# Low-rank products of an RWKV-7 layer in fp32 on two row tiles, two PSUM copies moved to ScalarE, and a new order of the whole layer

## The chip, the core and the metric

The kernel runs on one NeuronCore of a Trainium2 chip. The metric is the device time of one execution in microseconds. The kernel before took 1311.3 us as the median of 3 runs (1308.73 to 1313.69).

## What is computed

Two decoder layers run on one prompt of 512 tokens and on eight samples of 4 tokens, all in fp32, with weights shared by both. Layer 0, the one that the change touches, is RWKV-7 time mixing. Cut to what matters:

```python
proj = h @ w_in                                  # 1024 -> 8320 columns: r, k, v, wd, ad, z
xm = sh + (prev - sh) * mu                       # token shift
wf = w0 + jnp.tanh(wd) @ w2                      # low-rank product, 64 -> 2048
a = jax.nn.sigmoid(a0 + ad @ a2)                 # low-rank product, 64 -> 2048
decay = jnp.exp(-jnp.exp(-jax.nn.softplus(-wf) - 0.5))
# per head (32 heads of 64), token after token:
#   S = S*decay + (S @ -kk) (kk*a)^T + v k^T ;  y = S r
o = (groupnorm(y) + bonus) * jax.nn.silu(z)
out = o @ w_out
```

Layer 1 is a gated MLP (projections, a causal 128 by 128 mixing, an output projection); the change leaves it alone.

## The kernel before, in words

**Layout.** Features lie on partitions and tokens on columns. The 544 tokens are two halves of 272 columns (256 of the prompt and 16 of the samples, `HT`). Most fp32 products are made as three products of rounded halves (`mm3`, lines 249 to 252: high by high, high by low, low by high), each one TensorE instruction of 272 columns.

**Steps.** The 2048 mixer features are 16 tiles of 128 (two heads each). Step `p` of the loop projects k, r, v, z of tile `p`: four projections of 16 units, a unit being one `mm3`, so 64 units of three products a step (`units`, L375). Between the units stand the small products of the recurrence, taken from three tiles at once: low-rank products and Gram matrices of tile `p` or `p+1`, the chunk algebra of `p-1` (`lanes`, `merge`, `chain`, `sample`), the group norm of `p-2` (`tail`).

**The order is written out.** Each generator (`lora`, `kpost`, `chain`, ...) yields after each piece. The table `AT` (L1066) gives every piece a place `u`, counted in units from the start of its step; `agenda` sorts all pieces of all steps by `64 * p + u`, and inside the manual schedule every engine and the DMA queue of SP issue their instructions in exactly that order. A place of 115.1 thus means: in the step after, behind unit 51. `BANKS` says in which PSUM bank a product lands: `wa` is two banks used in turn, `sm`, `g`, `s`, `y` are one each; the projections have two of their own (`pp`), and a half of a projection can start only when the half before the last one has been read by ScalarE (`shift`, pieces 1 and 2, L392 and L393).

**What the change and the prediction touch.**

- `lora_in` (L413) rounds tanh(wd) and ad to high and low halves and stacks them on 128 partitions (`lw`, `la`). `lora(p)` (L432) loads the two 64 by 128 weights twice each, one copy below the other, rounds them (L442 on ScalarE), makes the low halves (L446, twice on VectorE), and then runs, for each half of the tokens and each of w and a, two products of 128 rows and 272 columns (L453, L454) with a tanh out of PSUM behind each pair (L457, L458). Pieces 11 to 14 are the `l1` copy, the VectorE scan L473, and the exponentials Ep and Em.
- `merge(p)` copies the product `pak` into ZR by VectorE (L752). `chain(p)` copies `pz` into XA in four pieces, two by VectorE (L843) and two by ScalarE (L841).
- `chain` then makes `pa` (L858) and `pn` (L864), adds the identity (L876), forms ND (L879) and RT (L885), and runs a serial loop of seven products `sb` (L889), each followed by one VectorE update of the state (L891) that the next one needs.
- `sample` has the products `psm` (L939 to L944), `pit` (L969), `psy` (L975) and `pst`/`psu` (L987): the last are two fp32 products of 64 rows and 256 columns on partitions 0 to 63 and 64 to 127. `gram` (L580) likewise pairs fp32 products of 64 rows and 128 columns.
- `flip` (L795) turns a block of the input for the residual; for its ninth call (k = 8) the sample rows are loaded.

Of the kernel before, what the change touches and what calls it, by code (L numbers as in the profile page):

```python
# [29 lines left out]
BANKS = {'plw0': 'wa', 'plw1': 'wa', 'pla0': 'sm', 'pla1': 'sm', 'pss': 'wa', 'pge0': 'y', 'pge1': 's', 'pgo0': 'wa', 'pgo1': 'wa', 'pbo0': 'sm', 'pbo1': 's', 'pbk0': 'wa', 'pbk1': 'wa', 'pv': 'wa', 'pat': 'sm', 'pak': 'y', 'pxt': 'wa', 'psu': 'wa', 'pm1': 'g', 'pm2': 's', 'pm3': 'wa', 'pm4': 'sm', 'ps0': 'wa', 'pit': 'wa', 'psy': 's', 'pst': 'sm', 'pso': 's', 'psm': 'wa'}  # L30
# [36 lines left out]
def build(tc, A, O, off):  # L67
# [5 lines left out]
    with ctx:  # L73
# [335 lines left out]
        lw = lH.tile([128, 2, HT], F32R, name="lw")  # L409
        la = lH.tile([128, 2, HT], F32R, name="la")  # L410
        xl = hd("xl", "h1")

        def lora_in():  # L413
            xlc, ll = (hd(n, t)[:, cl].rearrange("p (h j) -> p h j", h=2) for n, t in (("xlc", "h3"), ("ll", "h7")))
            parts = [(slice(0, 256), xl[:, 0:512].rearrange("p (h j) -> p h j", h=2)), (slice(256, 272), xl[:, 512:544].rearrange("p (h j) -> p h j", h=2))]
            for js, src in parts:
# [1123 lines left out]
```

## Time and profile before

| what | value |
|---|---|
| median of 3 runs | 1311.3 us (1308.73 to 1313.69) |
| the profiled execution, its own time | 1309.46 us |
| its span, first to last instruction | 1307.7 us |
| mean granted TensorE clock | 0.993 |
| TensorE matmul busy | 1266.9 us (97%) |
| VectorE busy | 991.5 us (76%) |
| ScalarE busy | 678.4 us (52%) |
| GpSimd busy | 158.4 us (12%) |
| DMA moved | 124.31 MB, mean 95 GB/s |

Busy shares are means over stages. The stage of the 16 steps fills the time from about 30 to 740 us; the output projection and layer 1 follow. Busy TensorE time counts the whole length of pipelined products, which overlap; the distance from one start to the next tells what a product costs in the stream. A row of the timeline ends, where the engine had been idle, with that idle time and what ended it, in brackets. TensorE's granted clock is 1.00 (2.4 GHz) except in a few short stretches at 0.50 (1.2 GHz).

### The profile page before, as it was taken

How to read it: one execution, taken by the hardware profiler on the slowest of the kernel's cores; microseconds unless marked ns; L12 is line 12 of the kernel's file. 1: busy time of each engine (PE TensorE's matmuls, PEld its weight loads, DVE VectorE, ACT ScalarE, POOL GpSimd, SP SyncE). 2: the span in 40 equal slices, each digit the busy share in tenths (PEclk: the TensorE clock that was granted, in tenths of full speed). 3: DMA queues.
4: the chain of work that ended last, by engine and by line, in shares of the span. 5: the costliest groups of instructions: out<-in, count | busy, mean ns of one | idle time of the engine just before them, and what ended most of it. 6: DMA issues, size and time to landing. Idle time of an engine off the chain costs nothing.

```text
span 1307.7 us, 35973 instructions
## 1 busy us (share of the span) xinstructions
PE 1266.9 (97%) x14860; PEld 1207.7 (92%) x14860; DVE 991.5 (76%) x2314; ACT 678.4 (52%) x1583; POOL 158.4 (12%) x350
## 2 busy tenths in 40 slices
PE   6989999999999999999999889999999999999997
PEld 5989999999999998999989779999999999999997
DVE  5779999999999998999989877374448656556466
ACT  5666576656766765666666453253333323233333
POOL 1112121121212111221212100000000000000000
PEclk9989999999999999999999999999999999999999
DMA  4424243434434342433323464433222232231511
GB/s 155 120 59 102 68 110 97 101 89 107 102 77 112 86 108 78 109 81 91 83 69 97 115 177 115 118 98 88 81 81 83 64 106 76 61 115 53 161 36 70
DMA packets 279785, 124.31 MB, mean 95 GB/s; under 512 B 114643, under 2 KB 272485, under 8 KB 279621
## 3 DMA queue, kind: packets, MB, share of 16 engines
q1 hardware_dynamic: 259972, 106.93, 30.5%
q10 hardware_dynamic: 19648, 15.08, 3.9%
q8 instruction: 117, 1.92, 0.6%
q14 instruction: 48, 0.39, 0.1%
HBM read 102.02 MB, written 19.95 MB: 93 GB/s over the span
## 4 chain that ended last, share of the span: by engine, by line
PE 71%; DVE 16%; ACT 6%; issue 3%; DMA 2%; POOL 2%; DVEq 0%; SPq 0%; POOLq 0%; ACTq 0%
PE r_p L250 3%; PE gz_p L250 3%; PE r_p L251 3%; PE r_p L252 3%; PE gz_p L252 2%; PE gu_p L250 2%; PE gz_p L251 2%; PE gu_p L252 2%; PE gu_p L251 2%; PE gv_p L251 2%; PE gv_p L252 2%; PE gv_p L250 2%; PE pgo L580 2%; PE po L250 2%; PE po L252 2%
## 5 line engine op out<-in xcount | busy, mean ns | idle before, releaser
L250 PE MATMUL r_p<-hh,r_h 128*128 128x272 f32 x256 | 79.4, 310 | 8.8 <-ACT raw L393 8.8
L395 POOL COPY shl<-raw 128x9 f32<-128x9 f32 x49 | 27.0, 552 | 497.8 <-ACT raw L393 487.8
L250 PE MATMUL z_p<-hh,z_h 128*128 128x272 f32 x256 | 80.3, 314 | 0.0
L250 PE MATMUL v_p<-hh,v_h 128*128 128x272 f32 x256 | 79.9, 312 | 0.0
L250 PE MATMUL k_p<-hh,k_h 128*128 128x272 f32 x256 | 77.6, 303 | 0.0
L250 PE MATMUL gv_p<-hh,gv_h 128*128 128x272 f32 x256 | 75.6, 295 | 0.0
L250 PE MATMUL gz_p<-hh,gz_h 128*128 128x272 f32 x256 | 75.5, 295 | 0.0
L251 PE MATMUL r_p<-hl,r_h 128*128 128x272 f32 x256 | 74.8, 292 | 0.0
L252 PE MATMUL r_p<-hh,r_l 128*128 128x272 f32 x256 | 74.7, 292 | 0.0
L252 PE MATMUL v_p<-hh,v_l 128*128 128x272 f32 x256 | 74.4, 291 | 0.0
L251 PE MATMUL v_p<-hl,v_h 128*128 128x272 f32 x256 | 74.3, 290 | 0.0
L250 PE MATMUL gu_p<-hh,gu_h 128*128 128x272 f32 x256 | 74.2, 290 | 0.0
L251 PE MATMUL gv_p<-hl,gv_h 128*128 128x272 f32 x256 | 74.2, 290 | 0.0
L252 PE MATMUL gv_p<-hh,gv_l 128*128 128x272 f32 x256 | 74.1, 289 | 0.0
L252 PE MATMUL k_p<-hh,k_l 128*128 128x272 f32 x256 | 74.0, 289 | 0.0
L251 PE MATMUL gu_p<-hl,gu_h 128*128 128x272 f32 x256 | 73.9, 289 | 0.0
L252 PE MATMUL gu_p<-hh,gu_l 128*128 128x272 f32 x256 | 73.9, 289 | 0.0
L252 PE MATMUL gz_p<-hh,gz_l 128*128 128x272 f32 x256 | 73.9, 289 | 0.0
L252 PE MATMUL z_p<-hh,z_l 128*128 128x272 f32 x256 | 73.8, 288 | 0.0
L251 PE MATMUL gz_p<-hl,gz_h 128*128 128x272 f32 x256 | 73.7, 288 | 0.0
L251 PE MATMUL k_p<-hl,k_h 128*128 128x272 f32 x256 | 73.7, 288 | 0.0
L251 PE MATMUL z_p<-hl,z_h 128*128 128x272 f32 x256 | 73.6, 288 | 0.0
(441 smaller groups left out, 4729.4 us busy)
## 6 DMA issues: line engine op xcount, KB each, us to landing
k_r<-rw_in SPq DMA_DIRECT2D x16, 512.0 KB
r_r<-rw_in SPq DMA_DIRECT2D x16, 512.0 KB
v_r<-rw_in SPq DMA_DIRECT2D x16, 512.0 KB
z_r<-rw_in SPq DMA_DIRECT2D x16, 512.0 KB
gv_r<-gm_in SPq DMA_DIRECT2D x16, 512.0 KB
gu_r<-gm_in SPq DMA_DIRECT2D x16, 512.0 KB
gz_r<-gm_in SPq DMA_DIRECT2D x16, 512.0 KB
go_r<-gm_out SPq DMA_DIRECT2D x24, 256.0 KB
```

The source lines that it names most:

```text
L250: T.matmul(ps, whi, ahi, start=first, stop=False)
L251: T.matmul(ps, whi, alo, start=False, stop=False)
L252: T.matmul(ps, wlo, ahi, start=False, stop=last)
L395: G.tensor_copy(shl[:, :, f], raw[:, 512:553:5])
L580: T.matmul(pg[h][:, 128 * j : 128 * j + 128], BK[rs, c].rearrange("p a b -> p (a b)"), AR[rs, :, c, :], start=True, stop=True)
```

## The change

The low-rank products become plain fp32: the weights are loaded once each, w2 on partitions 0 to 63 and a2 on 64 to 127, without rounding; for each half of the tokens one product of 64 rows and 272 columns is made for w and one for a, from the two row halves of TensorE into two banks. XA leaves PSUM by ScalarE alone, ZR too. All places and all banks of small products are new; the projections and everything after the steps stay as they were. The core of the diff (of the places, the lines that the prediction speaks of):

```diff
-BANKS = {'plw0': 'wa', 'plw1': 'wa', 'pla0': 'sm', 'pla1': 'sm', 'pss': 'wa', 'pge0': 'y', 'pge1': 's', 'pgo0': 'wa', 'pgo1': 'wa', 'pbo0': 'sm', 'pbo1': 's', 'pbk0': 'wa', 'pbk1': 'wa', 'pv': 'wa', 'pat': 'sm', 'pak': 'y', 'pxt': 'wa', 'psu': 'wa', 'pm1': 'g', 'pm2': 's', 'pm3': 'wa', 'pm4': 'sm', 'ps0': 'wa', 'pit': 'wa', 'psy': 's', 'pst': 'sm', 'pso': 's', 'psm': 'wa'}
+BANKS = {'plw0': 'wa', 'plw1': 'g', 'pla0': 'sm', 'pla1': 's', 'pss': 'g', 'pge0': 'g', 'pge1': 'wa', 'pgo0': 's', 'pgo1': 'wa', 'pbo0': 's', 'pbo1': 'g', 'pbk0': 'g', 'pbk1': 's', 'pv': 'y', 'pat': 'wa', 'pak': 'sm', 'pxt': 'sm', 'psu': 'wa', 'pm1': 'y', 'pm2': 'wa', 'pm3': 'sm', 'pm4': 'sm', 'ps0': 'wa', 'pit': 'wa', 'psy': 'sm', 'pst': 's', 'pso': 'wa', 'psm': 'y'}
...
-        lw = lH.tile([128, 2, HT], F32R, name="lw")
-        la = lH.tile([128, 2, HT], F32R, name="la")
+        lx = lH.tile([128, 2, HT], F32, name="lx")
         xl = hd("xl", "h1")
         def lora_in():
-            xlc, ll = (hd(n, t)[:, cl].rearrange("p (h j) -> p h j", h=2) for n, t in (("xlc", "h3"), ("ll", "h7")))
-            parts = [(slice(0, 256), xl[:, 0:512].rearrange("p (h j) -> p h j", h=2)), (slice(256, 272), xl[:, 512:544].rearrange("p (h j) -> p h j", h=2))]
-            for js, src in parts:
-                S.activation(xlc[e_, :, js], src[e_], AF.Tanh)
-            S.activation(lw[e_], xlc[e_], AF.Copy)
-            V.tensor_tensor(out=ll[e_], in0=xlc[e_], in1=lw[e_], op=ALU.subtract)
-            for js, src in parts:
-                S.activation(la[o_, :, js], src[o_], AF.Copy)
-                V.tensor_tensor(out=ll[o_, :, js], in0=src[o_], in1=la[o_, :, js], op=ALU.subtract)
-            for rs, os, x in ((e_, o_, lw), (o_, e_, la)):
-                S.activation(x[os], ll[rs], AF.Copy)
-            yield
-
-        lrls = [lH.tile([128, 2, 128], F32R, name=f"lrl{i}") for i in range(2)]
-        for x in lrls:
-            G.memset(x[o_, 0, :].bitcast(F32), 0.0)
-            G.memset(x[e_, 1, :].bitcast(F32), 0.0)
+            for js, src in ((slice(0, 256), xl[:, 0:512].rearrange("p (h j) -> p h j", h=2)), (slice(256, 272), xl[:, 512:544].rearrange("p (h j) -> p h j", h=2))):
+                S.activation(lx[e_, :, js], src[e_], AF.Tanh)
+                S.activation(lx[o_, :, js], src[o_], AF.Copy)
+            yield
         def lora(p):
             z = Z[p]
-            pb = slice(128 * p, 128 * p + 128)
-            lr = lH.tile([128, 2, 128], F32, name=f"lr{p}", tag="lr", bufs=1)
-            for i, n in enumerate(("rw_w2", "rw_a2")):
-                w = A[n][0, :, pb]
-                Q.dma_start(lr[:, i, :], bass.AP(w.tensor, w.offset, [[0, 2]] + [list(x) for x in w.ap]))
-            yield
-            lrh = lH.tile([128, 2, 128], F32R, name=f"lrh{p}", tag="lrh", bufs=2)
-            S.activation(lrh, lr, AF.Copy)
-            yield
-            lrl = lrls[p % 2]
-            for i, rs in enumerate((e_, o_)):
-                V.tensor_tensor(out=lrl[rs, i, :], in0=lr[rs, i, :], in1=lrh[rs, i, :], op=ALU.subtract)
-            yield
-            xa = z["xa"] = hd(f"xa{p}", "h1")
-            pw, pa = [None] * 2, [None] * 2
-
-            def down(h, i, x, ps):
-                ps[h] = bk(f"pl{'wa'[i]}{h}", p)[:, 0:HT]
-                T.matmul(ps[h], lrh[:, i, :], x[:, h, :], start=True, stop=False)
-                T.matmul(ps[h], lrl[:, i, :], x[:, h, :], start=False, stop=True)
-
-            def tanh(h, ps, dp_, ds_, bcol):
-                S.activation(dp_[:, 4 * h : 4 * h + 4, :], ps[h][:, 0:256].rearrange("p (c j) -> p c j", j=64), AF.Tanh, bias=bcol, scale=0.5)
-                S.activation(ds_[:, 4 * h : 4 * h + 4, :], ps[h][:, 256:272].rearrange("p (c j) -> p c j", j=4), AF.Tanh, bias=bcol, scale=0.5)
-
+            lr = lH.tile([128, 128], F32, name=f"lr{p}", tag="lr", bufs=2)
+            for n, rs in (("rw_w2", e_), ("rw_a2", o_)):
+                Q.dma_start(lr[rs], A[n][0, :, 128 * p : 128 * p + 128])
+            yield
             for h in range(2):
-                down(h, 0, lw, pw)
-                yield
-                tanh(h, pw, pv(xw), sv(xw), pcol(w0h, p))
-                yield
-                down(h, 1, la, pa)
-                yield
-                tanh(h, pa, cpv(xa), csv(xa), pcol(w0h, 16 + p))
-                yield
+                ps = [bk(f"pl{n}{h}", p)[:, 0:HT] for n in "wa"]
+                for x, rs in zip(ps, rw_):
+                    T.matmul(x, lr[rs], lx[rs, h, :], start=True, stop=True)
+                yield
+                if h == 0:
+                    xa = z["xa"] = hd(f"xa{p}", "h1")
+                for x, dp_, ds_, bcol in ((ps[0], pv(xw), sv(xw), pcol(w0h, p)), (ps[1], cpv(xa), csv(xa), pcol(w0h, 16 + p))):
+                    S.activation(dp_[:, 4 * h : 4 * h + 4, :], x[:, 0:256].rearrange("p (c j) -> p c j", j=64), AF.Tanh, bias=bcol, scale=0.5)
+                    S.activation(ds_[:, 4 * h : 4 * h + 4, :], x[:, 256:272].rearrange("p (c j) -> p c j", j=4), AF.Tanh, bias=bcol, scale=0.5)
+                    yield
...
-            V.tensor_copy(right(p)[:, :, 64:128], pk.rearrange("p (j k) -> p j k", k=64))
+            S.activation(right(p)[:, :, 64:128], pk.rearrange("p (j k) -> p j k", k=64), AF.Copy)
...
-                    if h:
-                        S.activation(XA[rs, h::2, :], c128(pz[a])[hs, :, 0:64], AF.Copy)
-                    else:
-                        V.tensor_copy(XA[rs, h::2, :], c128(pz[a])[hs, :, 0:64])
+                    S.activation(XA[rs, h::2, :], c128(pz[a])[hs, :, 0:64], AF.Copy)
...
-            sk=(14.7847, 15.8601, 16.324, 16.6354, 16.6354, 16.6354, 16.6354),
+            sk=(0.789221, 8.8031, 15.711, 15.8424, 17.6719, 17.7726, 18.4403),
-            bonus=(55.0395, 55.0395, 79.713, 79.713, 79.713, 79.713),
+            bonus=(47.1621, 50.0087, 67.1245, 68.9711, 69.0871, 71.7472),
-            sides=(73.8815, 76.9425, 82.4769, 90.6529, 90.874),
+            sides=(71.9966, 73.0768, 73.0768, 79.7128, 89.332),
-            lora=(-53.3437, -35.604, -22.0198, -6.51455, -6.51455, -5.67349, 1.68797, 1.68797, 5.54808, 5.54808, 6.00962, 7.83685, 9.52597, 14.6652, 14.6652, 18.0281),
+            lora=(-37.6497, -16.243, -12.6778, -6.32377, -6.32377, -5.15096, 0.12609, 0.958916, 8.84795, 19.5291, 19.5291, 39.8259),
-            merge=(80.6858, 90.1492, 90.1492, 91.3358, 93.8559, 94.4782, 95.4232, 98.4293, 102.797, 103.005, 103.005),
+            merge=(89.9516, 90.29, 91.6755, 91.6755, 93.2448, 94.0464, 94.0464, 99.0064, 99.0064, 102.136, 102.373),
-            smp=(12.838, 64.6761, 72.7011, 73.1509, 74.2051, 74.2051, 74.2051, 74.713, 75.2658, 76.703, 76.8464, 76.8464, 78.0988, 90.3058, 91.8793, 93.8484, 93.9934, 93.9934, 95.368, 98.3682, 100.668, 102.567, 110.18, 111.216, 111.216, 126.326, 133.839, 137.039, 155.339),
+            smp=(4.36649, 64.2531, 73.5271, 79.3115, 79.3115, 82.6169, 82.6169, 82.6169, 84.1463, 84.509, 88.3156, 89.5629, 89.5629, 90.1406, 90.873, 93.3779, 94.0364, 99.466, 102.52, 102.958, 103.396, 105.645, 115.209, 116.915, 116.947, 124.943, 129.788, 136.306, 191.625),
-            chain=(103.35, 103.492, 104.192, 104.192, 104.45, 104.45, 104.45, 106.129, 107.734, 110.12, 110.344, 110.344, 110.344, 110.344, 110.983, 110.983, 111.461, 111.99, 111.99, 116.223, 116.571, 118.245, 119.291, 120.662, 122.737, 122.737, 123.448, 124.261, 126.451, 128.474, 134.567, 137.125, 137.125, 137.16, 138.698, 138.698, 151.352, 196.182),
+            chain=(102.988, 102.988, 102.988, 102.988, 103.098, 104.998, 104.998, 105.819, 111.041, 111.599, 111.599, 111.599, 111.85, 111.85, 111.85, 114.008, 114.008, 114.008, 114.008, 115.066, 115.066, 115.284, 116.962, 118.608, 120.078, 121.408, 121.557, 123.546, 124.856, 128.208, 128.208, 129.056, 129.056, 129.056, 129.847, 129.965, 129.965, 147.17),
-            tail=(137.741, 139.93, 141.783, 143.235, 143.593, 146.755, 149.322, 152.651, 159.432, 160.601, 160.601, 163.12, 163.738, 163.738, 166.987, 169.754, 174.977, 174.977),
+            tail=(132.502, 132.502, 132.572, 132.98, 132.98, 141.147, 141.337, 146.854, 147.433, 159.083, 159.098, 163.745, 164.046, 166.048, 166.166, 166.34, 168.968, 171.692),
-            flip=(101.356, 103.429, 109.739, 165.658),
+            flip=(115.408, 135.41, 142.071, 165.144),
```

## Rows read from the trace of the kernel before

**Rows 1.** The profile page, part 1: the span, and the busy time and share of the span of each engine.

```profile
span 1307.7 us, 35973 instructions
PE 1266.9 (97%) x14860; PEld 1207.7 (92%) x14860; DVE 991.5 (76%) x2314; ACT 678.4 (52%) x1583; POOL 158.4 (12%) x350
```

**Rows 2.** Busy time by stretch (us from the span's start): length, then busy us and instructions of TensorE matmuls, weight loads, VectorE, ScalarE and GpSimd, the granted TensorE clock, the DMA share and GB/s. The first is a stretch of steps, the second of layer 1.

```profile
100.00:300.00 200.00, 197.91 (x2883) 186.34 (x2878) 182.76 (x464) 130.83 (x330) 39.10 (x82) 1.00 0.37 93
...
800.00:1000.00 200.00, 199.76 (x1585) 196.97 (x1585) 109.86 (x202) 73.14 (x146) 5.28 (x8) 1.00 0.32 91
```

**Rows 3.** Timeline of TensorE in a middle step, where the r projection starts: start in us, length in us, engine, line, operation, output and inputs, tile, count, and in brackets the idle time before and what ended it.

```profile
209.84 0.29 PE L614 MATMUL pbo<-rkh,bo 128*128 128x272 f32 x1
209.97 0.28 PE L615 MATMUL pbo<-rkl,bo 128*128 128x272 f32 x1
210.57 0.39 PE L250 MATMUL r_p<-hh,r_h 128*128 128x272 f32 x1 [0.32 <-ACT raw L393]
```

**Rows 4.** Waits over the whole span: engine and line, what was waited for, us in total, times, longest us.

```profile
ACT BT L949 <- DVE MM L947: 31.7, 16, 3.3
...
PE r_p L250 <- ACT raw L393: 8.8, 16, 3.5
```

**Rows 5.** Timeline of TensorE at the second step's r projection.

```profile
71.46 0.28 PE L615 MATMUL pbo<-rkl,bo 128*128 128x272 f32 x1
75.23 0.59 PE L250 MATMUL r_p<-hh,r_h 128*128 128x272 f32 x1 [3.49 <-ACT raw L393]
```

**Rows 6.** Timeline of VectorE just before that.

```profile
69.31 1.30 DVE L473 TENSOR_TENSOR_SCAN L<-cst,l 128x560 f32<-128x560 f32 x1
...
71.64 0.28 DVE L947 TENSOR_TENSOR MM<-psm,cst 128x128 f32<-128x128 f32 x1
```

**Rows 7.** Timeline of ScalarE in the same stretch: a copy out of the samples' PSUM tile, and the first copy out of the k projection.

```profile
71.96 0.28 ACT L949 ACTIVATE BT<-psm 128x128 f32<-128x128 f32 x1 [3.28 <-DVE MM L947]
...
74.74 0.37 ACT L392 ACTIVATE raw<-k_p 128x256 f32<-128x256 f32 x1
```

**Rows 8.** Busy time by stretch, columns as in rows 2, for the two stretches of the steps behind a long idle time of TensorE.

```profile
75.00:80.30 5.30, 5.07 (x22) 5.07 (x23) 3.89 (x7) 4.71 (x10) 1.81 (x4) 0.50 0.76 200
...
500.20:503.60 3.40, 3.21 (x15) 3.15 (x16) 2.25 (x6) 1.60 (x6) 0.00 (x0) 0.53 0.71 182
```

**Rows 9.** Timeline of TensorE at the ninth call of flip.

```profile
500.39 0.63 PE L811 MATMUL pxt<-cst,xr 32*128 32x32 f32 x4 [1.82 <-DMA xr<-x_sample]
```

**Rows 10.** Timeline of TensorE in the first step, at its low-rank products and its r projection.

```profile
38.13 0.39 PE L453 MATMUL pla<-la,lrh 128*128 128x272 f32 x1 [0.54 <-ACT xa L458]
...
40.28 0.39 PE L250 MATMUL r_p<-hh,r_h 128*128 128x272 f32 x1 [0.89 <-ACT raw L393]
```

**Rows 11.** Timeline of TensorE in a step, at the first product of the pair pst and psu.

```profile
143.58 0.48 PE L987 MATMUL pst<-We,BT 64*128 64x256 f32 x1
```

**Rows 12.** Timeline of TensorE one step later, at the same pair, with the first product behind it.

```profile
188.16 0.48 PE L987 MATMUL pst<-We,BT 64*128 64x256 f32 x1
188.16 0.48 PE L987 MATMUL psu<-We,BT 64*128 64x256 f32 x1
188.48 0.38 PE L987 MATMUL pst<-We,BT 64*128 64x256 f32 x1
...
188.79 1.15 PE L864 MATMUL pn<-W,GK 128*64 128x64 f32 x32
```

**Rows 13.** Timeline of TensorE in the Gram products: the second and the last of sixteen pairs (each pair is a record of pgo and one of pge; the row of pgo is shown), and what follows.

```profile
225.61 0.27 PE L580 MATMUL pgo<-AR,BK 64*128 64x128 f32 x1
...
227.18 0.27 PE L580 MATMUL pgo<-AR,BK 64*128 64x128 f32 x1
...
227.38 1.16 PE L835 MATMUL pz<-ZR,Zf 64*64 64x128 f32 x32
```

**Rows 14.** Timeline of TensorE around one lone small product of the chain.

```profile
192.49 0.29 PE L252 MATMUL z_p<-hh,z_l 128*128 128x272 f32 x1
192.61 0.33 PE L889 MATMUL sb<-RS,MB 128*128 128x64 f32 x2
192.75 0.37 PE L250 MATMUL z_p<-hh,z_h 128*128 128x272 f32 x1
192.96 0.29 PE L251 MATMUL z_p<-hl,z_h 128*128 128x272 f32 x1
```

**Rows 15.** Groups of instructions of VectorE over the span: line, operation, tiles, shapes, count, busy us, mean ns of one, idle time before.

```profile
L891 DVE SCALAR_TENSOR_TENSOR RS<-sb,D,ND 128x64 f32<-128x64 f32 x112 | 31.1, 278 | 2.9 <-PE sb L889 2.3
L843 DVE COPY XA<-pz 64x256 f32<-64x256 f32 x32 | 13.3, 417 | 1.7
L608 DVE TENSOR_TENSOR rkl<-rk,rkh 128x544 fp32r<-128x544 f32 x16 | 11.6, 724 | 1.9 <-DMA od<-of 1.9
L752 DVE COPY ZR<-pak 128x512 f32<-128x512 f32 x16 | 10.9, 681 | 2.6 <-PE pak L747 2.6
L446 DVE TENSOR_TENSOR lrl<-lr,lrh 64x128 fp32r<-64x128 f32 x32 | 9.1, 283 | 0.5
```

**Rows 16.** The same of ScalarE.

```profile
L841 ACT ACTIVATE XA<-pz 64x256 f32<-64x256 f32 x32 | 12.2, 380 | 21.1 <-DVE XA L843 20.0
L670 ACT ACTIVATE ZR<-pat 128x512 f32<-128x512 f32 x16 | 9.6, 599 | 3.2 <-PE pat L668 3.2
L442 ACT ACTIVATE lrh<-lr 128x256 fp32r<-128x256 f32 x16 | 6.5, 408 | 0.0
```

More of the change, by code (lines that the diff above doesn't have):

```diff
@@ L493, in kpost @@
             AR = z["AR"] = l0.tile([128, 2, NCH, 64], F32, name=f"AR{p}", tag="AR", bufs=2)
-            V.tensor_tensor(out=AR[:, 0], in0=cpv(u), in1=pe(Ep), op=ALU.mult)
+            V.tensor_tensor(out=AR[:, 0], in0=cpv(u), in1=pe(z["Ep"]), op=ALU.mult)
             yield
             AS = z["AS"] = lH.tile([128, 2, 32], F32, name=f"AS{p}", tag="AS", bufs=2)
-            V.tensor_tensor(out=b4(AS[:, 0, :]), in0=csv(u), in1=se(Ep), op=ALU.mult)
+            V.tensor_tensor(out=b4(AS[:, 0, :]), in0=csv(u), in1=se(z["Ep"]), op=ALU.mult)
             yield
@@ L502, in kpost @@
             ua = hd(f"ua{p}", "h7")
-            V.scalar_tensor_tensor(out=ua[:, cl], in0=xa[:, cl], scalar=1.0, in1=u[:, cl], op0=ALU.add, op1=ALU.mult)
+            V.scalar_tensor_tensor(out=ua[:, cl], in0=z["xa"][:, cl], scalar=1.0, in1=u[:, cl], op0=ALU.add, op1=ALU.mult)
             yield
             k2 = z["k2"] = hd(f"k2_{p}", "h8")
-            S.activation(k2[:, cl], xa[:, cl], AF.Identity, scale=pcol(kah, p), bias=pcol(ka1, p))
+            S.activation(k2[:, cl], z["xa"][:, cl], AF.Identity, scale=pcol(kah, p), bias=pcol(ka1, p))
             yield
@@ L550, in rpost @@
             z = Z[p]
-            AR, AS, Ep, k2, r = (z[n] for n in ("AR", "AS", "Ep", "k2", "r"))
+            AR, AS, Ep, r = (z[n] for n in ("AR", "AS", "Ep", "r"))
             V.tensor_tensor(out=AR[:, 1], in0=cpv(r), in1=pv(Ep), op=ALU.mult)
@@ L556, in rpost @@
             rk2 = z["rk2"] = hd(f"rk2{p}", "h1")
-            V.scalar_tensor_tensor(out=rk2[:, cl], in0=r[:, cl], scalar=pcol(RK, p), in1=k2[:, cl], op0=ALU.mult, op1=ALU.mult)
+            V.scalar_tensor_tensor(out=rk2[:, cl], in0=r[:, cl], scalar=pcol(RK, p), in1=z["k2"][:, cl], op0=ALU.mult, op1=ALU.mult)
             yield
@@ L1075, in build @@
-            lin=(9.80119,),
-            kpost=(19.9275, 21.9207, 23.6166, 23.9847, 23.9847, 23.9847, 28.9781, 28.9781, 30.0807, 30.4572, 49.3099),
-            norms=(29.8797, 29.8797, 31.3932, 43.1277, 43.3032, 43.3032),
-            norms0=(27.863, 27.863, 31.1422, 33.3135, 41.7292, 52.9902),
-            rpost=(34.7435, 38.6104, 38.7431, 62.3877),
-            gram=(39.0376, 39.0376, 39.0376, 39.0376, 39.0376, 40.2945, 44.0649, 44.5579, 47.5737),
-            vpost=(59.4074,),
-            bonus=(55.0395, 55.0395, 79.713, 79.713, 79.713, 79.713),
@@ L1088, in build @@
-            lanes=(39.112, 59.2551, 59.2551, 59.4273, 61.5138, 61.6685, 62.9447, 62.9447, 62.9447, 62.9447, 62.9447, 69.5511, 69.8722, 69.8722, 69.8722, 70.0168, 70.0168, 70.2336, 70.9978, 71.1188, 74.7254, 74.7254),
-            merge=(80.6858, 90.1492, 90.1492, 91.3358, 93.8559, 94.4782, 95.4232, 98.4293, 102.797, 103.005, 103.005),
-            smp=(12.838, 64.6761, 72.7011, 73.1509, 74.2051, 74.2051, 74.2051, 74.713, 75.2658, 76.703, 76.8464, 76.8464, 78.0988, 90.3058, 91.8793, 93.8484, 93.9934, 93.9934, 95.368, 98.3682, 100.668, 102.567, 110.18, 111.216, 111.216, 126.326, 133.839, 137.039, 155.339),
@@ L1093, in build @@
-            flip=(101.356, 103.429, 109.739, 165.658),
+            wk=(-24.6703, -13.9502, -10.5009),
+            wr=(-1.92923, 4.85448, 5.61825),
+            wv=(0.606097, 15.3323, 15.3323),
+            wz=(26.5557, 37.8471, 43.6636),
+            sk=(0.789221, 8.8031, 15.711, 15.8424, 17.6719, 17.7726, 18.4403),
+            sr=(7.54549, 28.6206, 31.674, 31.674, 34.0009, 34.0009, 38.5955),
+            sv=(43.7782, 45.1654, 47.4232, 49.7307, 49.7307, 51.0746, 55.203),
+            sl=(-48.6951, -2.31874, 1.08412, 4.68622, 4.68622, 4.68622, 4.68622),
@@ new lines, in build @@
+            lin=(5.21945,),
+            kpost=(24.9494, 25.986, 25.986, 25.986, 26.4478, 26.4478, 26.4478, 28.1479, 28.7234, 28.9758, 46.1589),
+            norms=(26.5963, 27.2646, 42.3595, 42.3595, 43.7228, 43.7228),
+            norms0=(30.3638, 36.1029, 36.1029, 42.7321, 43.0652, 43.81),
+            rpost=(34.2118, 40.034, 43.0665, 59.6417),
+            gram=(38.5207, 38.5207, 38.5207, 38.5207, 38.5507, 38.7256, 44.4019, 46.8335, 55.0017),
+            vpost=(57.36,),
+            bonus=(47.1621, 50.0087, 67.1245, 68.9711, 69.0871, 71.7472),
@@ new lines, in build @@
+            gate=(58.7304, 58.7304, 68.9911, 70.1851, 70.432, 104.018),
+            keys=(51.7578, 52.1495, 90.6263, 93.0718),
+            sides=(71.9966, 73.0768, 73.0768, 79.7128, 89.332),
+            lora=(-37.6497, -16.243, -12.6778, -6.32377, -6.32377, -5.15096, 0.12609, 0.958916, 8.84795, 19.5291, 19.5291, 39.8259),
+            lora0=(-48.6977, 9.64576, 9.64576, 9.68669, 9.68669, 9.68669, 9.68669, 9.68669, 9.69389, 18.8347, 22.6537, 30.7022),
+            lanes=(4.59191, 56.0959, 56.1972, 56.1972, 57.7957, 57.8272, 57.8272, 59.1798, 61.4444, 61.4444, 61.7838, 61.7838, 63.4843, 63.4843, 64.0257, 64.7786, 65.5865, 65.5865, 68.1234, 68.1534, 76.599, 78.8691),
```

13 lines of the change are left out of this document (2 added, 11 removed).

## The prediction

> **What bounds the kernel now.** Part 1 of the page comes first: TensorE is busy for 97% of the span, VectorE for 76% [rows 1]. Busy time by stretch then parts the stages: in 200 us of steps TensorE is busy for 197.9, VectorE for 182.8, ScalarE for 130.8; in layer 1 only TensorE is full [rows 2]. The timeline shows what TensorE's share means: 272-column products start 0.125 us apart (209.84 to 209.97), with nothing between. Its one regular hole is ahead of the r projection, which starts 0.60 us after the product before it instead of 0.125 [rows 3], so 0.48 us a step, 16 times, until ScalarE has read the first half of k [rows 4]. The table of places says why: that copy (`sk`, piece 1) has place 15.86, just ahead of unit 16, and stands in ScalarE's queue behind Ep, Em and the samples' copy BT, which itself waits for VectorE 16 times, 31.7 us in all [rows 4].
>
> In the second step the hole is 3.77 us [rows 5]. VectorE runs the low-rank scan from 69.31 and reaches MM at 71.64 [rows 6]; BT has then waited 3.28 us, and the copy of k starts at 74.74 [rows 7]. Behind the hole TensorE is granted 0.50 of its clock, the 1.2 GHz level, up to 80.3. The other slow stretch of the steps, 500.2 to 503.6 at 0.53 [rows 8], also follows a hole, 1.82 us for the DMA of the sample rows in the ninth flip [rows 9]. The first step has two holes of 0.54 and 0.89 us, at its low-rank products and at r [rows 10]. A step lasts 143.58 to 188.16, 44.58 us [rows 11, 12]. So the steps are bound by TensorE's stream, with VectorE close behind; what is put into the stream is paid, and what leaves VectorE pays only where TensorE waited for it.
>
> **The change, part by part; first TensorE in one step.**
>
> The eight rounded products leave: 8 x 0.125 = 1.00 us less [rows 3].
>
> Two pairs of fp32 products of 64 rows come. The nearest row is pst with psu, of 256 columns. Both start at 188.16, so they do run side by side; each product is two records, and the next product starts at 188.79: 0.63 us for the pair [rows 12]. Sixteen more columns cost little: in the Gram products fourteen pairs of 128 columns take 225.61 to 227.18, 0.112 us each [rows 13], so 16 columns in two passes add 0.03. That is 0.66 a pair, 1.32 a step. The TensorEngine Tiling page of the Trainium skill gives a factor of up to 2 for a contract dimension of 64 (Theoretical Speedup), which read as a whole factor would be 2 x 2 x 0.238 = 0.95 us a step and put the total some 5.5 us lower. Its section Key Properties says that changing the tiling mode drains the engine, which speaks against this change, and pst is the row of this case that bears it out. I take pst, because its price holds the edges: 0.63 is well over the 0.45 that 2 x 256 columns cost at the pace inside the Gram products.
>
> The places move nearly all small products into other gaps. I cut both tables into the groups that fall between two units. A lone `sb` shows what a gap costs: 0.14 us for itself, and the product behind it needs 0.21 instead of 0.125 [rows 14]; leaving a 64-row group for another kind costs about 0.09 too (the last Gram pair takes 0.20 instead of 0.112 [rows 13]). Before, 14 groups of small products interrupt the units, after, 13. But psm and pat get a gap of their own (about +0.1), `sb` 7 and 4 meet column- or row-tiled products (+0.1 each, and +0.05 behind the second pair), pst stands between two `sb` (+0.1), psy between the Gram products and pz (+0.1), the second and third pit no longer share a gap (+0.1), while pit 1 ahead of pm1, and pyt behind pit 3, save about 0.15. The sum is +0.5, an estimate from these edges; bounds 0 and +0.8.
>
> The hole at r: `sk` piece 1 moves from 15.86 to 8.80, seven units ahead of its use: -0.48. Ep and Em move behind it, to 19.53, and are first read near 26.
>
> New waits. `sk` 2, the copies of v and of z stand 1.5 to 8 units ahead of their use. Tight are: `sb` 2, in one gap with `sb` 1 and only pst (0.63) between, while VectorE's queue has the bonus subtraction (0.72 us) ahead of the state update (0.28) [rows 12, 15]; `sb` 7, behind the lanes; and the first pit, which waits through GR (a ScalarE copy of the sample's products) for a ScalarE queue that now also holds ZR. Behind each of them on TensorE stands every projection product, so a wait there is paid in full. Bounds -0.1 (a cover now unseen) and +0.8 a step (one late bonus subtraction); I take +0.15, near the low end, since the same chain runs today without a regular hole.
>
> Sum for a step: -1.00 + 1.32 + 0.50 - 0.48 + 0.15 = +0.49 us, times 15 = **+7.3 us**.
>
> VectorE loses two lrl (0.57), ZR (0.68) and two XA pieces (0.83), 2.1 us of some 41 a step [rows 15]; it gives TensorE nothing but the holes counted here. ScalarE gains ZR (0.60) and two XA pieces (0.76) and loses lrh (0.41), +0.95 us [rows 16]. The cover is its own idle third [rows 2], and it no longer waits 20.0 us in all for VectorE's half of XA [rows 16]; without the cover the copies of the projections would come late and TensorE would stand for up to 0.95 a step, which lies in the rivals' range.
>
> Queues. On SP the weights w2 and a2 are loaded once instead of twice, still two issues, ahead of z's load. The flip's load moves 20 units ahead of its product instead of 2. The sample state's store goes behind the Gram diagonals, its buffer is reused 8 units later. The norms' second hop stays behind the first. None is waited for closely. GpSimd moves its small copies (D from 18.0 to 39.8, used a step later) and is busy 12%: nothing. The four memsets and the roundings of `lora_in` leave the start.
>
> **Once, not per step.** First step: the holes of 0.54 and 0.89 come from the low-rank chain, now shorter and behind k's copy: -1.4 (bounds -1.6, 0). Second step: the hole goes, 3.64 less the 0.48 counted above, 3.16, and the 5.3 us at half clock, worth 2.65 [rows 5, 8]. In its place VectorE, bound by lanes and scan as before, is next late for the first pit: +1.5, an estimate from 1.30 of scan, two roundings and the samples' chain. Net -4.3 (bounds -5.8, 0). Ninth flip: -1.8 and half of 3.4 us: -3.5 [rows 8, 9]. The end of the steps and layer 1: 0 (bounds -4, +3). Sum: **-9.2 us**.
>
> In all -1.9 us on the execution profiled, 1309.46: 1307.6. That run lies 1.8 us under the median shown, so the forecast as a median is **1309.4 us**.
>
> **Rivals.** *The edges are hidden.* If regrouping costs nothing, a step gains or loses almost nothing (-0.01) and the single holes decide: -9.3, 1302.0. For it: one group less. Against: every edge seen has its 0.09. By the skill's whole factor it would be about 1296.
>
> *VectorE's queue at the chain, the slow side.* `sb` 2 and the next `sb` wait each step for the update behind the bonus subtraction: +0.65 more a step, +9.8, so 1319.2. Point of decision: RT ending later than about 0.1 us ahead of `sb` 1. For it: the gap from pa to `sb` 1 shrinks from six units and two groups to four units and two shorter ones. Against: VectorE has 2 us less to do.
>
> *The holes only move.* The second step's hole and its half clock stay in another place: +4.3 and, with the flip's, +7.8: 1317.2 at most.
>
> *The pairs do not run side by side.* Each would take about 0.48 more, 1.0 a step: 1324. Pst and psu starting together exclude it nearly.
>
> **How the numbers follow.** Forecast 0.40, edges hidden 0.27 (some 0.05 of it the whole factor), VectorE's queue 0.25, moved holes 0.06, no side by side 0.02. A measurement of this kernel tells about 0.5%, 6.6 us, from no change. Faster takes the second case and a little of the first, 0.29; slower the third, part of the fourth and the last, 0.30; same 0.41. The range runs from between the two faster prices, 1298, to 1322, past the slow rival.
>
> **What would show it.** Right: no idle time left of r projection on ScalarE's raw copy beyond 0.1 us; pairs pla and plw starting together, 0.66 to the next line; a step about 45 us; no stretch at half clock near 75 or 500; ScalarE without waits on XA. Wrong: a step under 44.3 (edges), or a new hole ahead of `sb`, py or pit on VectorE in every step, or idle of ScalarE's making ahead of a projection.

## The result and the profile after

The kernel after takes 1300.7 us (median of 4 runs, 1299.1 to 1303.1), the kernel before beside it 1312.3 us (1308.7 to 1313.7): ratio 0.9918, interval 0.9896 to 0.9941. Forecast were 1309.4 us and a range of 1298 to 1322. The execution profiled is the slowest of the four, 1303.13 us.

Part 1 of the page after, and the totals of part 4, the chain that ended last:

```profile
span 1301.3 us, 35878 instructions
PE 1272.5 (98%) x14860; PEld 1200.1 (92%) x14860; DVE 961.2 (74%) x2231; ACT 690.9 (53%) x1612; POOL 126.6 (10%) x346
...
PE 90%; ACT 5%; DVE 2%; DMA 1%; issue 1%; POOL 0%; SPq 0%; ACTq 0%; POOLq 0%; DVEq 0%
```

TensorE's busy time grew by 5.6 us [rows 1] while the span fell by 6.4. Busy time by stretch (TensorE, weight loads, VectorE, ScalarE, GpSimd; then the granted clock), the steps first, then the places of the two old stretches at half clock, the second step and the ninth flip:

```profile
100.00:300.00 200.00, 199.56 (x2855) 184.31 (x2854) 174.91 (x441) 135.24 (x340) 31.13 (x86) 1.00 0.36 94
800.00:1000.00 200.00, 199.76 (x1585) 196.81 (x1585) 111.78 (x207) 73.77 (x147) 3.49 (x7) 1.00 0.32 92
75.00:80.30 5.30, 5.30 (x160) 4.82 (x159) 4.67 (x13) 4.27 (x10) 0.00 (x0) 1.00 0.72 202
514.00:519.00 5.00, 5.00 (x45) 4.81 (x44) 4.93 (x12) 3.72 (x10) 0.55 (x3) 1.00 0.11 14
```

TensorE now works 199.56 of 200 us in the steps (197.91 before [rows 2]), and both places have the full clock [rows 8]. What TensorE still waits for, by the waits view (us in total, times, longest):

```profile
PE psy L940 <- ACT Zf L761: 1.2, 1, 1.2
PE pgo L548 <- DVE AR L520: 1.1, 1, 1.1
PE sb L854 <- DVE RS L850: 0.9, 1, 0.9
```

`pgo` falls into the first step, `sb` into the last, psy behind the steps; from the second step to the last but one nothing stops TensorE by more than 0.13 us. The row of r waiting for ScalarE's raw copy, 8.8 us over 16 times [rows 4], is gone.

The ledger of the two profiled executions, by the starts of the first k product of each step. The first of them comes 0.7 us later, the first step is unchanged (31.94 to 31.98), the second falls from 46.59 to 41.48, **-5.1**. Regular steps **grow**, from 44.58 to 45.03 with a flip and from 44.35 to 44.61 without, +5.1 over 13 steps. The step with the ninth flip falls from 48.28 to 45.37: -3.4 beside the regular growth. Four steps of before were 0.7 to 2.1 us over the regular one, none after: **-4.2**. The last step is 0.2 longer, all behind the steps 0.3. Sum -6.4. So TensorE's stream costs more, as forecast, and stalls of before pay for it. The medians lie 5 us further apart than these two executions: the one of after is 2.4 us above its median, the one of before (1309.46) 2.9 us under its. What fills these 5 us is not shown.

### The profile page after: what moved, and what is told of

Read it like the earlier page. It is cut to its first block, busy times and chain, and to the rows that moved or that the text cites. A ratio compares the mean times of both kernels' runs of the same rounds, so it can differ in the third digit from the quotient of the medians.

```text
span 1301.3 us, 35878 instructions
## 1 busy us (share of the span) xinstructions
PE 1272.5 (98%) x14860; PEld 1200.1 (92%) x14860; DVE 961.2 (74%) x2231; ACT 690.9 (53%) x1612; POOL 126.6 (10%) x346
## 4 chain that ended last, share of the span: by engine, by line
PE 90%; ACT 5%; DVE 2%; DMA 1%; issue 1%; POOL 0%; SPq 0%; ACTq 0%; POOLq 0%; DVEq 0%
PE z_p L250 3%; PE gz_p L250 3%; PE k_p L250 2%; PE gz_p L252 2%; PE k_p L252 2%; PE k_p L251 2%; PE gz_p L251 2%; PE gu_p L250 2%; PE gu_p L252 2%; PE gu_p L251 2%; PE gv_p L251 2%; PE gv_p L252 2%; PE gv_p L250 2%; PE r_p L250 2%; PE z_p L252 2%; PE z_p L251 2%
## 5 line engine op out<-in xcount | busy, mean ns | idle before, releaser
L250 PE MATMUL v_p<-hh,v_h 128*128 128x272 f32 x256 | 76.7, 299 | 0.0
```

Source lines behind the costliest of these rows:

```text
L250: T.matmul(ps, whi, ahi, start=first, stop=False)
```

## Experiments

Steps are measured from the first k product of one to that of the next, with / without a flip in them. One run alone has no interval.

| kernel | median us | ratio to before (95%) | regular step | second step |
|---|---|---|---|---|
| before | 1312.3 | | 44.58 / 44.35 | 46.59 |
| after | 1300.7 | 0.9918 (0.9896 to 0.9941) | 45.03 / 44.61 | 41.48 |
| e1 | 1311.5 | 0.9987 (0.9965 to 1.0009) | 44.17 / 43.97 | 46.67 |
| e2 | 1336.6 | 1.0174 (1.0150 to 1.0199) | 47.1 to 50.0 / 44.38 | 47.30 |
| e3 | 1335.9 | 1.0172 (1.0148 to 1.0195) | 46.6 to 49.8 / 44.05 | 45.29 |
| e2b | 1312.6 | one run | 45.3 to 47.3 / 44.38 | 46.52 |
| e8 | 1308.5 | 0.9965 (0.9948 to 0.9983) | 44.17 / 43.95 | 43.96 |
| e9 | 1304.4 | 0.9950 (0.9932 to 0.9968) | 44.17 / 43.95 | 44.10 |
| e4 | 1319.4 | 1.0046 (1.0032 to 1.0061) | 45.21 / 45.00 | 46.29 |
| e5 | 1297.6 | 0.9882 (0.9843 to 0.9920) | 44.63 / 44.20 | 40.86 |
| e6 | 1302.7 | 0.9923 (0.9898 to 0.9947) | 45.02 / 44.58 | 42.87 |
| e11 | 1308.3 | one run | 45.50 / 45.07 | 41.47 |
| e10 | 1326.6 | one run | 44.58 / 44.43 | 46.55 |
| e13 | 1296.3 | 0.9879 (0.9856 to 0.9902) | 44.64 / 44.21 | 40.85 |

**e1, one hole closed by one place.**

```diff
-sk=(14.7847, 15.8601, 16.324, ...
+sk=(0.789221, 8.8031, 16.324, ...
```

> The kernel before with one edit: the copy of k's projection out of PSUM gets the places of the kernel after (sk pieces 0 and 1 from 14.78 and 15.86 to 0.79 and 8.80); low-rank products, banks and all other places stay. Theory (holes in TensorE's stream made the gain): the start distance ahead of the r projection falls from 0.60 to 0.125 us, a regular step from 44.58 to 44.10, and the second step loses its 3.77 us hole and the 6.8 us at half clock behind it; 14 x 0.48 and 3 to 6 us make -10 to -13 us, ratio 0.990 to 0.992. Rival (VectorE's queue binds, and the hole only moves): the same time is lost ahead of pit, sb or the chain, the step stays at 44.4 to 44.6, total within 3 us of before. Rival (the fp32 pairs or ScalarE's copies made the gain): also near before, since none of them is in.

The regular step fell by 0.41, close to the theory, some 5 us in all; the total hardly. The first step grew by 2.4 us, and the steps with odd stalls stood 7.7 us over the regular one instead of 4.2 (some of them are those of e10). In the first step the copy of k now stands ahead of the low-rank inputs in ScalarE's queue, and TensorE waited 2.4 us there instead of at r. And the second step's hole broke up (timeline of TensorE, rows with idle time):

```profile
75.23 0.39 PE L252 MATMUL r_p<-hh,r_l 128*128 128x272 f32 x1 [0.49 <-DVE r_l L372]
79.63 0.39 PE L250 MATMUL r_p<-hh,r_h 128*128 128x272 f32 x1 [1.38 <-ACT raw L393]
82.06 0.36 PE L746 MATMUL pm<-T,GK 64*64 64x64 f32 x1 [1.03 <-DVE T L736]
```

Two of the three wait for VectorE. The transpose T on it (STREAM_TRANSPOSE), here and in the kernel after:

```profile
81.31 0.70 DVE L736 STREAM_TRANSPOSE T<-Zf 128x512 f32<-128x512 f32 x1
```

```profile
75.33 0.71 DVE L704 STREAM_TRANSPOSE T<-Zf 128x512 f32<-128x512 f32 x1
```

They start 15.9 and 12.0 us after the step's start: two of the three waits hang on VectorE's queue, and the new order brings T 4 us earlier.

**e2 and e3, the flip's places alone, and with e1's edit.**

```diff
-flip=(101.356, 103.429, 109.739, 165.658)
+flip=(115.408, 135.41, 142.071, 165.144)
```

> The kernel before with one edit: the four places of flip are those of the kernel after, so each load of the residual's block stands 20 units ahead of its transposes instead of 2. Theory (holes): only the ninth call changes, its 1.82 us wait for the sample rows and the 3.4 us at half clock behind it go, -3.5 us, ratio 0.997, and the step of 48.28 us becomes about 45.2 as its neighbours. Rival (the load is late for another cause, such as the DMA queue's order): the wait stays at 1 to 2 us in its new place, total unchanged.

> The kernel before with both edits, k's copy early and flip early; eight rounded low-rank products, VectorE's copies and all other places as before. Theory (holes): the two gains add, -13 to -17 us, 1295 to 1299, so below the kernel after, whose steps pay 0.3 to 0.45 us each for pairs and edges. Rival (VectorE's queue): no more than the flip's -3.5 us. If the pairs or the relief of VectorE were what the change earned by, this kernel stays well above the kernel after (1301).

Both missed: instead of gaining 3.5 and 13 to 17 us, they are 23 us slower than the kernel before. The ninth flip's wait went, but a wait of 2.34 us came into nearly every step with a flip (e2: waits, and the timeline around one of them):

```profile
PE pv L661 <- DVE m L1023: 21.3, 9, 2.6
```

```profile
306.64 0.44 PE L939 MATMUL psm<-AD,BD 128*128 128x128 f32 x2
...
311.56 0.28 DVE L962 SCALAR_TENSOR_TENSOR GR<-psm,cst,GR 128x64 f32<-128x64 f32 x1
311.76 0.16 DVE L1023 TENSOR_SCALAR m<-m 128x9 f32<-128x9 f32 x1
...
311.99 0.63 PE L661 MATMUL pv<-cst,xv 128*128 128x128 f32 x4 [2.34 <-DVE m L1023]
```

`m` is no operand of pv; it is VectorE's next instruction behind GR, the last reader of psm. ScalarE reads pxt only at 313.25, so until then pxt holds one of the two banks `wa`, and pv is left with psm's.

**e2b, the same with pxt in bank `sm`.**

```diff
-'pxt': 'wa'
+'pxt': 'sm'
```

> The run with all four places of flip early, with one more edit: the transposes pxt land in bank sm, as in the kernel after, instead of one of the two banks wa. That run lost 2.34 us in every step with a flip, ahead of pv. Theory (pxt took its turn in wa between psm and pv, so pv was given psm's bank, which VectorE and ScalarE still read): the waits of pv go, a regular step is 44.4 to 44.7, the ninth flip's wait and the half clock behind it go as well, -3 to -5 us against the kernel before, 1307 to 1310. Rival (the transposes' new place itself makes pv late, by the copy of pxt in ScalarE's queue or the group norm's means): steps stay at 47 to 48.

The waits of pv are gone: the bank was the cause. But the copy of pxt now stands ahead of k's copy on ScalarE, the hole at r is 0.70 us instead of 0.32 in those steps, and by the one run nothing is gained in all, against 3 to 5 us expected.

**e8 and e9, three local edits.** Both: e1's edit, and

```diff
-wr=(-18.1685, ...
+wr=(-16.5, ...
-flip=(101.356, 103.429, 109.739, 165.658)
+flip=(88.5, 103.429, 109.739, 165.658)     # e8
+flip=(101.356, 103.429, 109.739, 165.2)    # e9
```

> The kernel before with three local edits of places: k's copy early as in the first run (sk 0.79, 8.80); only the load of flip early (101.36 to 88.5), its transposes and copies where they were; and the load of r's weights (wr piece 0, -18.17 to -16.50) behind the store of the mixer's output on SP instead of ahead of it. In the kernel before VectorE waited 3 times, 1.9 us in all, and in the first run 4 times, 4.0 us, for that store ahead of rkl, and sb of TensorE behind it. Theory (each stall has its own local cause): regular step 44.17, no wait of rkl for the store, the ninth flip's 2.0 us and its half clock gone: -6 to -9 us against the first run, 1303 to 1306; the second step keeps its stall. Rival (a stall that is removed comes back at the next late thing): no more than -3 us against the first run, 1308 to 1312.

> The kernel of the run before (k's copy early, r's weights behind the store of the mixer's output) with flip's load back at 101.36 and, instead, flip's store a little earlier (165.66 to 165.20), so that SP issues the store of block k-1 ahead of the loads of block k. In the kernel before the two loads of the ninth call were issued 8.2 us apart, and with the earlier load 18.7 us apart, the second each time right behind the transposes of the first. Theory (the block still to be stored holds one of the two buffers, so the second load waits for the transposes of the first): with the store first both loads are issued together, the wait of 1.8 us and the half clock behind it go, 51.7 us of that step become 45 to 48, -3 to -6 us in all. Rival (the sample rows land late for DMA traffic): the wait stays at 1.8 us, no change.

VectorE's wait for the mixer's store, 4.0 us in e1, is in neither. (The kernel after loads r's weights later still, at -1.93, also behind that store.) e8's total missed the 1303 to 1306 expected, as it left the ninth flip's wait at 1.79 us; e9, with the total as expected, took it. SP's issues show why (start, us from the first to the last of a row), e8 and then e9:

```profile
481.77 19.01 SPq L803 DMA_DIRECT2D xr<-x_sample  x2
...
504.70 0.44 SPq L818 DMA_DIRECT2D xfd<-xo  x1
```

```profile
488.88 0.44 SPq L818 DMA_DIRECT2D xfd<-xo  x1
489.36 2.98 SPq L803 DMA_DIRECT2D xr<-x_sample  x2
```

The second row of e8 shows the store last: the second load of e8 is held until the first block has been transposed, since the unstored block keeps the other buffer. With the store first the step falls from 51.7 to 45.0 us. Of these 6.7 us, 1.8 are the wait, 0.9 a stall of the kind of e10 (1.2 us in e8, 0.3 in e9), 0.4 a wait of sb, and 3.5 the clock: for the same 667 products TensorE is busy for 47.99 us at a mean of 0.93 in e8 and for 44.49 at 1.00 in e9. A load that is merely issued earlier gains nothing.

The second step of e8 is 2.7 us shorter than that of e1, though TensorE waits in it at the same three products (0.48, 1.37 and 1.04 us, in e1 0.49, 1.38 and 1.03). Busy time by stretch of the whole second step, e1 and then e8:

```profile
65.41:112.09 46.68, 43.67 (x586) 40.84 (x584) 37.43 (x96) 27.68 (x69) 6.53 (x18) 0.93 0.31 75
```

```profile
64.93:108.89 43.96, 40.97 (x586) 38.24 (x585) 37.27 (x96) 27.56 (x69) 6.52 (x18) 1.00 0.32 79
```

For the same 586 products TensorE is busy 2.70 us longer in e1, whose clock is 0.50 from the third wait on (81.5 to 88.3), while in e8 it stayed at 1.00. So these 2.7 us of the second step are the clock alone. Since the waits are the same, nothing in e8's edits is known to have kept it up.

**e4 and e5, the pairs on the old places, the rounded products on the new.** e4 is the kernel before with the new `lora_in` and `lora`; e5 the kernel after with the old ones, each half's w and a products in one piece:

```diff
 # e4, table of before
-lora=(-53.3437, -35.604, -22.0198, -6.51455, -6.51455, -5.67349, 1.68797, 1.68797, 5.54808, ...
+lora=(-53.3437, -5.67349, -5.67349, 1.68797, 5.54808, ...
 # e5, table of after
-lora=(-37.6497, -16.243, ...
+lora=(-53.3437, -35.604, -22.0198, -16.243, ...
```

> The kernel before with the low-rank products of the kernel after (two fp32 pairs on row tiles a step, no roundings) at the old places: the first pair where the a product of half 0 stood, the second where that of half 1 stood; all else as before, the hole at r included. Theory (pairs cost more than they save): -1.00 for the eight rounded products, +0.66 to 0.80 a pair, so +0.3 to +0.6 us a step, 44.9 to 45.2 for the regular step, +4 to +9 us in all. Rival (pairs cheap, a whole factor of two from the row tiles): -0.05 us a step, total -1 to 0. Rival (VectorE's relief of 0.57 us a step counts): the waits for k's copy and sb shrink, a step of 44.3 or less.

> The kernel after with the eight rounded low-rank products of the kernel before (w and a of one half in one piece, at the two places of the fp32 pairs; weights loaded twice each, lrh on ScalarE and two lrl on VectorE again; ScalarE's copies and all other places as after). Theory (the new places removed the stalls, and the fp32 pairs are a cost): a regular step falls from 45.03 to about 44.4 us, as the pairs added 0.63 on the old places, no stall returns, -8 to -10 us against the kernel after, 1290 to 1293. Rival (the pairs earn by taking work off VectorE, ScalarE and the queues): with 0.57 us more on VectorE and 0.4 on ScalarE a step, waits come back ahead of sb or a projection, and the total is that of the kernel after or more, 1300 to 1310. Rival (pairs and rounded products cost the same): 45.0 a step, 1300.

The pairs cost 0.63 us a step on the old places and 0.41 on the new. One of them in the kernel after, and the rounded four at the same place of e5 (timeline of TensorE):

```profile
235.96 0.33 PE L854 MATMUL sb<-RS,MB 128*128 128x64 f32 x2
236.22 0.49 PE L428 MATMUL plw<-lx,lr 64*128 64x272 f32 x1
236.23 0.49 PE L428 MATMUL pla<-lx,lr 64*128 64x272 f32 x1
236.55 0.39 PE L428 MATMUL plw<-lx,lr 64*128 64x272 f32 x1
236.56 0.39 PE L428 MATMUL pla<-lx,lr 64*128 64x272 f32 x1
236.88 0.39 PE L250 MATMUL z_p<-hh,z_h 128*128 128x272 f32 x1
237.11 0.29 PE L251 MATMUL z_p<-hl,z_h 128*128 128x272 f32 x1
```

```profile
234.61 0.33 PE L886 MATMUL sb<-RS,MB 128*128 128x64 f32 x2
234.76 0.37 PE L453 MATMUL plw<-lw,lrh 128*128 128x272 f32 x1
...
235.34 0.28 PE L250 MATMUL z_p<-hh,z_h 128*128 128x272 f32 x1
235.46 0.29 PE L251 MATMUL z_p<-hl,z_h 128*128 128x272 f32 x1
```

From `sb` to the second product behind: 1.15 and 0.85 us. The two halves do run side by side, and from the pair's start to the next product it is 0.66 us, as forecast. The rounded products have the full array's shape and add no edge to that of `sb`. e5's step is 0.41 us shorter than that of the kernel after, without any relief of VectorE by the pairs. Its median is 3.1 us lower, not the 8 to 10 expected; the pairs' places give back less than the 0.63 counted on, and the first step is 1.3 us longer, as TensorE waits there for the roundings (1.34 us ahead of plw).

**e6, ZR and half of XA by VectorE again** (both lines of the diff undone).

> The kernel after with ZR and half of XA copied by VectorE again, as in the kernel before; pairs, banks and places as after. Theory (places): nothing waits for these copies closely, the step stays at 45.0 us, total within 2 us of the kernel after, 1299 to 1303. Rival (VectorE's relief carries the gain): 1.5 us more on VectorE a step bring waits back ahead of sb, pit or the rounded weights, +0.2 us or more a step, 1304 to 1312.

Steps as after, to 0.03 us, but for one of 45.35: the relief of VectorE is worth nothing there. The second step alone is 1.4 us longer, with pm waiting 1.33 us for T. T in turn waited for a transfer and not for VectorE's copies:

```profile
76.72 0.71 DVE L704 STREAM_TRANSPOSE T<-Zf 128x512 f32<-128x512 f32 x1 [1.30 <-DMA Zf<-dz]
```

The load of Zf was issued at 71.43 to 72.69 us, in the kernel after at 71.36 to 72.62, where T did not wait at 75.33. Why it landed later in e6 is open, and whether the copies have a part in it is not shown.

**e11, one group moved to a gap of its own.**

```diff
-norms=(26.5963, 27.2646, ...
+norms=(27.6, 27.6, ...
```

> The kernel after with the four products pss moved one unit on, from the gap behind unit 26, which they share with pit, the first pm and pak, to a gap of their own behind unit 27. Theory (every gap has its edges, 0.085 us on either side of products of another shape): the regular step grows from 45.03 to 45.15 to 45.20 us. Rival (edges are hidden, a group costs only its products): 45.03.

+0.47 us a step, against 0.12 to 0.17 expected; e11 is one run, but all its regular steps are alike. The two gaps account for +0.20 (from 2.20 to 1.85 and 0.56, each over what the units around take); the rest, 0.28, came where nothing was moved, in the Gram products. First pairs and last of one step, after:

```profile
220.33 0.37 PE L548 MATMUL pgo<-AR,BK 64*128 64x128 f32 x1
220.34 0.37 PE L548 MATMUL pge<-AR,BK 64*128 64x128 f32 x1
220.54 0.27 PE L548 MATMUL pgo<-AR,BK 64*128 64x128 f32 x1
220.55 0.27 PE L548 MATMUL pge<-AR,BK 64*128 64x128 f32 x1
...
222.31 0.43 PE L940 MATMUL psy<-W,MM 128*128 128x64 f32 x2
```

and in e11:

```profile
220.92 0.37 PE L548 MATMUL pgo<-AR,BK 64*128 64x128 f32 x1
221.11 0.34 PE L548 MATMUL pge<-AR,BK 64*128 64x128 f32 x1
221.14 0.38 PE L548 MATMUL pgo<-AR,BK 64*128 64x128 f32 x2
221.29 0.27 PE L548 MATMUL pge<-AR,BK 64*128 64x128 f32 x1
...
223.18 0.43 PE L940 MATMUL psy<-W,MM 128*128 128x64 f32 x2
```

The first pair no longer starts together, and the sixteen pairs take 2.26 us instead of 1.98, in 14 of the 16 steps alike. Why `pge` starts late is open.

**e10, 64 more small products ahead of the steps.**

```diff
-T.transpose(pt[:, so_ : so_ + 32], xsh[:, ks], ident[0:32, 0:32])
+for _ in range(5):
+    T.transpose(pt[:, so_ : so_ + 32], xsh[:, ks], ident[0:32, 0:32])
```

> The kernel before with the 16 transposes of the sample rows at the start each made five times, so 64 more products (128 more instructions with their weight loads) on TensorE ahead of all steps, where it is idle a third of the time; everything in the steps as before. The waits of TensorE for nothing that the profile shows stand at instructions number 6593 and 18625 of its stream in the kernel before, and at 6593, 11969, 13249 and 18625 in the three later kernels with the old order: all are 193 above a multiple of 256, and 117 instruction transfers of 16 KB fit 256 instructions each. Theory (TensorE runs out of instructions at block borders inside the dense stretches of small products): the waits at pss in the sixth and the fifteenth step are gone, as the border falls 128 instructions earlier in the program; any such wait left is again 193 above a multiple of 256, at other products; -2 to +2 us in all. Rival (pss itself waits, for its bank or its operand): the waits stay at pss in the same two steps.

TensorE's waits for nothing that the profile shows, in e9 (old order) and in e10:

```profile
PE pss L532 <- issue: 2.7, 2, 1.5
PE r_p L251 <- issue: 0.6, 1, 0.6
PE pm L759 <- issue: 0.3, 1, 0.3
```

```profile
PE pm L760 <- issue: 1.3, 2, 1.1
PE pss L533 <- issue: 0.7, 1, 0.7
PE r_p L253 <- issue: 0.6, 1, 0.6
```

Counted from zero in order of start, with weight loads and the sequencer's records, the first instructions behind e9's four waits stand at instructions 6593, 11969, 13249 and 18625, behind e10's at 4033, 9409, 14785 and 16065: all 193 above a multiple of 256, at other steps than before. So they belong to blocks of the instruction stream, not to pss; in no kernel with the new places do they cost more than 0.2 us. Why the new order escapes them was not tried. The total missed: the added products cost 9.6 us, 0.15 each, because TensorE was not idle there but full (in the kernel before 10.00 of the 10 us from 20 to 30).

**e13, e5 with the first step's low-rank products later.**

```diff
-lora0=(-149.921, -5.42802, 0.549203, 9.64576, 9.64576, 9.68669, ...
+lora0=(-149.921, -5.42802, 0.549203, 13.1, 13.1, 13.1, ...
```

> The kernel of the run with the eight rounded low-rank products on the new places, with one more edit: in the first step alone its low-rank products stand at 13.1 instead of 9.65, so that the rounding ahead of them is done (TensorE waited 1.34 and 0.30 us for it). Meant as the version faster than both kernels. Theory: regular step 44.62 us as before this edit, the two waits gone, -1 to -1.6 us, a median of 1295 to 1297.5, some 4 us under the kernel after. Rival (the first step is bound by VectorE's chain to the Gram products, whose wait of 1.1 us then grows by what is saved): unchanged, 1297 to 1298.

The rival was right about the first step: 33.25 to 33.19 us, as pss, v and pgo now wait (0.56, 0.38 and 1.36 us). It is not told apart from e5, but at 1295.97 to 1296.57 us all its runs lie under all of the kernel after.

## Why the prediction was right, and where it was not

The time lies in the range, 8.7 us under the point, and the change is faster by 0.6 to 1.0%, where I had held no measurable change likeliest (0.41) and given faster 0.29. Where the gain lies is shown by three runs: the pairs alone cost 6 us (e4), the new order without the pairs gains 15 (e5), and the copies put back on VectorE change the total by 2 us, inside the noise (e6).

- **The regular step** was forecast at +0.49 and measured +0.45 with a flip, +0.26 without. Its terms: pairs for rounded products +0.32 forecast, +0.41 on the new places (e5); edges of regrouping +0.50 forecast, +0.46 / +0.25 (e5 against e8, which differ in little else inside a regular step); the hole at r -0.48, measured -0.41 (e1); new waits +0.15, none. The +0.66 a pair came as read from pst and psu [rows 12]; what was short is the edge behind it. The TensorEngine Tiling (Array Packing) page of the Trainium skill says that changing the tiling mode drains TensorE (Key Properties). The runs do not part such a drain from any other edge: behind a row-tiled pair the next product needs 0.23 us instead of 0.125, but behind a lone `sb`, which has the full array's shape, also 0.21 [rows 14]. Nor does pst bear it out, as I had read: of its 0.63 us 0.32 lie between its own two records, where no mode changes [rows 12], so its price is not that of edges. The same page gives a factor of up to 2 for a contract dimension of 64 (Theoretical Speedup). By the pace of the Gram pairs [rows 13] the whole factor would give an estimated 0.48 us a pair, and it takes 0.66, 0.33 for each of its two records; why is open.
- **The second step**: -4.3, and half a microsecond of the regular growth, forecast; -5.1 measured. The new wait of 1.5 us that I put in its place did not come. The term for the clock, 2.65, is borne out by e1 against e8, 2.70. e1 shows that k's copy alone was no cure for the waits. That VectorE's new order is one is argued from when T starts (12.0 instead of 15.9 us into the step); no run has that order alone.
- **The ninth flip**: -3.5 forecast, -3.4 measured, for the wrong reason. The wait was not a load issued too late but one held back for a buffer (e8, e9).
- **The first step**: -1.4 forecast, nothing measured, and 0.7 us lost ahead of it. The time went to the Gram products' wait for VectorE, 1.1 us.
- **The step that failed** is "new waits", which counted only what the change adds. The odd stalls of before, 4.2 us of the profiled execution, went too: VectorE's wait for the mixer's store ahead of `rkl`, with `sb` behind it (closed alone by e8's SP edit), and TensorE's block stalls (e10). Steps of 45.3 and 46.4 us stood in the trace of before; I took one step of 44.58 for all.
- **The rivals**: *edges hidden* gave 1302.0, nearest to the time, but its mechanism is excluded by e11. *VectorE's queue at the chain* did not come: no `sb` waits but one of 0.9 us in the last step. *The holes only move* was right of each edit made alone (e1, e2b, e8) and wrong of the whole set.
- **What would show it**: r without idle time, pairs together and 0.66 long, a step of 45, full clock near 75 and 500, all as said. ScalarE still waits at XA, now for TensorE's pz (33.4 us in all instead of 20.0 for VectorE [rows 16]), and nobody waits for that.

## What to carry to other kernels

In an order written out by hand a place is bound to its neighbours in three ways, the bank rotation, the buffer count and the queue: move one alone and its stall mostly reappears, so set them together and judge each part by the length of a regular step, which tells 0.05 us where a total tells 3; and look at the granted clock of a step before giving its length a cause, since the same waits came with 2.7 us of half clock in one run and none in another. Count what stalls irregularly before, step by step, since an order that clears these earns more than the edit it came with. A cheaper form in products is not one in time: eight products of the full array's shape beat four on two row tiles, and the new places with the old products are the fastest kernel here (e13).

## What the runs showed of the hardware

- TensorE's stream stops at a fixed phase of its instructions, 193 above a multiple of 256, for 0.2 to 2.1 us, at two to four places in an execution of the old order. The page's 117 instruction transfers of 16 KB fit that: its 29,720 TensorE instructions make 254 for each, an estimate that takes them all for TensorE's.

```profile
q8 instruction: 117, 1.92, 0.6%
```

- Such a stop can cost more than itself: behind the one of 1.48 us of e9 the mean clock of 7 us is 0.76 (TensorE's busy time and clock by stretch), so part of it ran at the 1.2 GHz level. It need not: behind one of 1.35 us in e1 the clock stays at 1.00, as behind the three waits of e8's second step. What decides it is open.

```profile
665.00:672.00 7.00, 6.49 (x74) 6.11 (x75) 3.77 (x9) 3.57 (x11) 2.71 (x8) 0.76 0.02 4
```

```profile
266.00:271.00 5.00, 4.77 (x72) 4.46 (x73) 3.48 (x9) 3.30 (x10) 2.35 (x7) 1.00 0.29 88
```

- Two streams of row-tiled products that start 0.19 us apart lose 0.28 us over sixteen pairs (e11). In the first step of the kernel after they start 0.20 apart and lose 0.16, so the distance at the start is not all of it.
